# RWKV in lockstep: the results of four pairs kept in SBUF up to their group norms, and the recurrences placed later among the dense products

## The chip, the cores and the metric

The kernel runs on one core of a Trainium2 chip. Its engines work side by side, each through its own queue in order: PE (TensorE, the matmuls; its weight loads are a separate row, PEld), DVE (VectorE), ACT (ScalarE), POOL (GpSimd) and SP (SyncE, which here only issues DMA transfers). PE's clock has two levels, 1.2 and 2.4 GHz; the trace gives the granted clock as a share of the higher one. The metric is the device time of one execution in microseconds (us).

## The reference

A sequence of 512 tokens of width 1024 passes a first network of two layers and then this block: RWKV-7 and a chunked state-space mixer (SSD) side by side, gates that merge the two, and a mixture of 32 experts. The change lies in the RWKV mixer. Its core, cut:

```python
def rwkv7_mix(p, ...):                      # 16 heads of 64
    ...                                     # r, k, v, decay w, kk, a, gate g
    def step(state, inp):
        r_t, w_t, k_t, v_t, kk_t, a_t = inp
        sa = jnp.einsum('bhij,bhj->bhi', state, -kk_t)
        state = (state * w_t[:, :, None, :]
                 + sa[..., None] * (kk_t * a_t)[:, :, None, :]
                 + v_t[..., None] * k_t[:, :, None, :])
        return state, jnp.einsum('bhij,bhj->bhi', state, r_t)
    _, ys = lax.scan(step, state0, xs)
    y = jnp.moveaxis(ys, 0, 1)
    mean = jnp.mean(y, axis=-1, keepdims=True)            # group norm, per head
    var = jnp.mean(jnp.square(y - mean), axis=-1, keepdims=True)
    y = ((y - mean) * lax.rsqrt(var + RWKV_GN_EPS)).reshape(B_, S_, RWKV_WIDTH)
    y = y * ln_g + ln_b
    bonus = jnp.sum(r_h * k_h * r_k, axis=-1, keepdims=True) * v_h
    return (y + bonus.reshape(B_, S_, RWKV_WIDTH)) * g

def second_block(x, ...):
    proj = rmsnorm(x, attn_norm_g) @ w_in
    y_a, y_b = rwkv7_mix(...), ssd_mix(...)
    gates = jax.nn.sigmoid(p_gate)                        # g_a, g_b
    x = x + (g_a * (y_a @ w_up_rwkv) + g_b * (y_b @ w_up_ssd)) @ w_out
    x = x + hier_moe(rmsnorm(x, ffn_norm_g), ...)         # 32 experts, top 2
    return rmsnorm(x, final_norm_g)
```

## The kernel before

Stages of the program, by the trace's time: the first network up to about 1290 us; the two mixers (class Mix) to 2133; the merge, which multiplies their results with w_up_ssd and w_up_rwkv and then w_out, to 2330; the experts to the end.

**What a dense product is.** All activations lie transposed, 128 channels x 512 tokens. A dense product of 128 output channels is 24 matmuls of 128x512 on the rows L219 to L221 (three for each of eight slices: the operands are split into a high and a low part, on ACT, L174 and L177, and DVE, L175 and L178). Its raw weights come by a DMA of 512 KB (L193, tile wr). A gate product (G, function gate) is one such product, then DVE and ACT (L1367, L1368) and a store of gates.

**Mix.run** walks the string PLAN (L788), one step after the other: L, T set-ups; A and B, the two preparations of a pair of RWKV heads (prep1, prep2; each head pair is 128 channels, eight pairs in all); C, the recurrence of four pairs at once (chain; C0 for pairs 0 to 3, C4 for 4 to 7); P, preparation of a group of SSD heads; U, an SSD unit; V, an SSD unit with a gate product set between its parts; G, a gate product; F, fetching ahead for the merge of w_up_ssd's weights and of SSD's results (tile yr, multiplied by rs on POOL, then split as x on ACT and DVE). From this program order a scheduler makes each engine's order by dependences and free buffers, so neighbouring steps are interleaved. Inside chain, PE's own order is written by hand (manual_schedule).

**A preparation's result** is tile CH (one buffer), which prep2 stores to the DRAM scratch ch (2304 KB, L1068). GA, another tile, holds products of prep1's Gram matrices for prep2.

**chain** (L1070) runs two halves, a and b, of two pairs each, in turn through eight chunks of 64 tokens. Each half and chunk loads its slice of ch into a tile CS (576 KB, four buffers, L1095), runs groups of eight 64x64 matmuls (L1090), copies out U (L1107) and SA (L1115), and makes the next state S (L1127). The chunk's output is copied on ACT to the tile ye (L1130) and stored to DRAM as yraw (L1131).

**close** (L1133), four times behind the chain, is the group norm of one pair: y is loaded back from yraw (L1139), PE sums it over each head with the matrix bdones (L1142), DVE subtracts the mean (L1143), ACT squares into gs (L1145), PE sums again (L1147), ACT takes the root (L1149), DVE the reciprocal (L1150), two DVE steps apply ln_g, ln_b and the bonus bo (L1151, L1152; bo is loaded at L1140), then gs takes the gate g from DRAM (lora, L1154), POOL multiplies (L1155), and the result is stored as ya (L1156). The buffers of each tile are numbers in the table SB2; y and gs have one each, PSUM's cb, which both sums use, has one.

Of the kernel before, what the change touches and what calls it, by code (L numbers as in the profile page):

```python
# [8 lines left out]
F32 = mybir.dt.float32  # L9
# [681 lines left out]
AR, GK, GB, VT, BT, KT, MM = (slice(a, a + n) for a, n in ((0, 128), (128, 128), (256, 64), (320, 64), (384, 64), (448, 64), (512, 64)))  # L691
# [29 lines left out]
def pack2(x):  # L721
# [7 lines left out]
    for n in ("w_up_rwkv", "w_up_ssd", "rwkv_w_decay", "rwkv_w_a", "rwkv_w_g"):  # L729
# [5 lines left out]
    return I  # L735


SB2 = dict(k=1, r=1, v=1, L=1, E2=1, th=1, kk=1, kp=1, bo=2, y=1, gs=1, eC=3,
           CH=1, CS=4, GA=1, inv=5, N=1, M=1, Tt=1, tmp=2, U=2, SA=2, S=4, Se=2, ye=3,
           bg=5, x=2, z=1, gt=1, bt=1, xdt=1, xw=1, prev=1, G=3, e=1, ys=1, acc=1, selp=2, tp=2)  # L740
PS2 = dict(d=2, ga=2, X=1, cb=1, sb=2)

# [42 lines left out]
    return r  # L785


PLAN = "L0 L1 T A0 L2 P B0 V V A1 U B1 U P A2 V B2 V A3 U B3 V P C0 A4 V B4 U V A5 B5 U P A6 V B6 V A7 B7 U U G G C4 G G G F G F G F"  # L788


ON = dict(kk1="a", kkn="v", kp1="a", kp2="v", b="v", bK="v", inv="v", NB="a", Se="v", yg="p", cv="a", G0="v", G1="v",
# [3 lines left out]
class Mix:  # L795


    def __init__(self, K, norm, V, coef, scr, ya, yb, rs, gates):
        self.K, self.nc, self.norm, self.V = K, K.nc, norm, V
        self.ya, self.yb, self.rs, self.gates = ya, yb, rs, gates  # L800
        nc, I = K.nc, K.I
        two = (128, 2, 64)
        K.place(bg=(128, 512), bt=(128, 512), gt=(128, 512), y=(128, 512), gs=(128, 512), bo=(128, 512),
                kp=(128, 512), U=two, SA=two, S=two, Se=two, ye=two)
        K.place(CH=(128, 8, 576), CS=(128, 2, 576), GA=(128, 8, 64))
        def cst(name, shape, src=None):
            t = K.c(name, shape)
            nc.sync.dma_start(t, I["c_" + name] if src is None else src)
            return t
        self.bdones = cst("bdones", (128, 128))  # L810
        self.gmask = cst("gmask", (128, 128))
        self.lev = cst("lev", (128, 3, 64))
        self.id16 = cst("id16", (64, 256))
        self.scr = scr
        for n, t in coef.items():
            setattr(self, n, t)
        self.gps = []
        for i in range(2):
            t = K.c(f"gp{i}", (128, 514))
            nc.vector.memset(t[:, 0:1], 0.0)  # L820
            self.gps.append(t)
        self.gqs = []
        for i in range(2):
            t = K.c(f"gq{i}", (128, 515))
            nc.vector.memset(t[:, 0:3], 0.0)
            self.gqs.append(t)
        self.E1 = K.c("E1", (128, 8, 65))
        nc.vector.memset(self.E1[:, :, 0:1], 1.0)


        self.ch = [K.dr.tile([8, 2, 128, 2, 576], F32, name=f"ch{i}") for i in range(2)]
        self.eC = [[K.c(f"eC{i}{j}", (128, 2, 8)) for j in range(2)] for i in range(2)]
        self.yr = [K.dr.tile([4, 128, 512], F32, name=f"yraw{i}") for i in range(2)]
        self.bon = K.dr.tile([1024, 512], F32, name="bonus")
        self.lo = [K.dr.tile([1024, 512], F32, name=f"lora{i}") for i in range(3)]

# [93 lines left out]
    def prep1(self, p):  # L930
# [38 lines left out]
        self.proj(16 + p, ev("v", 16 + p))  # L969
        CH = P["CH"] = K.t("CH", (128, 8, 576))  # L970
        for i in range(2):
# [14 lines left out]
    def prep2(self, p, P):  # L986


        K, nc = self.K, self.nc
        CH, E2, th, kp, v = (P[n] for n in ("CH", "E2", "th", "kp", "v"))  # L990
# [17 lines left out]
                for a in range(2):  # L1008
                    self.scaled("tr", t[part(h), :, a, :], ps[part(a), :, part(h)])
        nc.vector.tensor_mul(th, th, E2)  # L1010
        GA = K.t("GA", (128, 8, 64))
        for i in range(2):
            ps, c4 = gram(th, i), slice(4 * i, 4 * i + 4)
            nc.vector.tensor_mul(GA[:, c4, :], ps[:, :, 0:64], gm[:, :, 0:64])
# [5 lines left out]
        N = K.t("N", (64, 16, 16))  # L1020
# [6 lines left out]
        M = K.t("M", (64, 16, 16))  # L1027
        nc.vector.tensor_copy(M, self.id16.rearrange("p (s t) -> p s t", s=16))
        for t in range(15, 0, -1):
            n = 16 - t  # L1030
# [4 lines left out]
        Tt = K.t("Tt", (64, 16, 16))  # L1035
# [34 lines left out]
    def chain(self, G):  # L1070


        with self.K.tc.manual_schedule(engines={mybir.EngineType.PE}):
            a, b = self.half(G, 0), self.half(G, 1)
            for c in range(8):
                for g in (a, b, a, a, b, a, b, b) if c else (a, a, a, b, a, b, b):
                    next(g)
            next(b)
        for n in range(4):
            self.close(4 * G + n)  # L1080

    def half(self, G, g):

        K, nc = self.K, self.nc
        part = lambda h: slice(h * 64, h * 64 + 64)
        def mm(o, st, mv, start=False, stop=False):
            for n in range(2):
                for h in range(2):
                    q = part(h)
                    nc.tensor.matmul(o[q, n, :], st[q, n, :], mv[q, n, :], start=start and not n, stop=stop,  # L1090
                                     skip_group_check=True)
        two = (128, 2, 64)
        for c in range(8):
            x = K.t("CS", (128, 2, 576))
            nc.sync.dma_start(x, self.ch[G][c, g])  # L1095
            at = lambda s: x[:, :, s]
            ARA, ARR, GKA, GKR = (at(slice(n, n + 64)) for n in (0, 64, 128, 192))
            eC = self.eC[G][g][:, :, c:c + 1].to_broadcast([128, 2, 64])

            X, Y = (K.p(t, (128, 2, 2, 64)) for t in (("cb", "X"), ("d", "d"))[g])  # L1100
            mm(X[:, 0], GKA, at(VT), True, not c)
            if c:
                mm(X[:, 0], ARA, S, stop=True)
            if c < 7:
                mm(X[:, 1], at(KT), at(VT))
            U = K.t("U", two)
            nc.vector.tensor_copy(U, X[:, 0])  # L1107
            yield
            mm(Y[:, 0], at(VT), GKR, True)
            if c:  # L1110
                mm(Y[:, 0], S, ARR)
            yield
            mm(Y[:, 1], at(MM), U, stop=True)
            SA = K.t("SA", two)
            nc.vector.tensor_copy(SA, Y[:, 1])  # L1115
            yield
            if c < 7:
                mm(X[:, 1], at(BT), SA, stop=True)
            mm(Y[:, 0], SA, at(GB), stop=True)
            if c < 7:  # L1120
                Sn = K.t("S", two)
                if c:
                    Se = K.t("Se", two)
                    nc.vector.tensor_add(Se, X[:, 1], S)
                    nc.vector.tensor_mul(Sn, Se, eC)
                else:
                    nc.vector.tensor_mul(Sn, X[:, 1], eC)  # L1127
                S = Sn
            y = K.t("ye", two)
            nc.scalar.copy(y, Y[:, 0])  # L1130
            nc.sync.dma_start(self.yr[G][2 * g:2 * g + 2, :, c * 64:(c + 1) * 64].rearrange("n p t -> p n t"), y)  # L1131
            yield

    def close(self, p):

        K, nc, V = self.K, self.nc, self.V
        col = lambda t: t[:, p:p + 1]
        y, bo = K.t("y"), K.t("bo")
        nc.sync.dma_start(y, self.yr[p // 4][p % 4])  # L1139
        nc.sync.dma_start(bo, self.bon[p * 128:(p + 1) * 128, :])  # L1140
        ps = K.p("cb")
        nc.tensor.matmul(ps, self.bdones, y, start=True, stop=True)  # L1142
# [10 lines left out]
        g = K.t("gs")  # L1153
# [903 lines left out]
```

## Time and profile before

| what | value |
|---|---|
| median of three runs | 2842.55 us (2842.48 to 2857.47) |
| the profiled execution, whole | 2841.89 us |
| its span in the trace | 2840.1 us |
| mean granted clock of PE | 0.978 |
| PE busy in the span | 2677.9 us (94%) |
| DVE, ACT, POOL busy | 60%, 37%, 7% |
| DMA moved | 504.44 MB, 178 GB/s on average |

A row of the timeline has the start, the duration, the engine, the line of the kernel, the operation and its tiles (out<-in), and in brackets how long the engine stood idle before it and what released it. DMA rows on SPq are the issue only, not the transfer. The windows give busy time of each engine in a stretch, the granted clock (1.00 is 2.4 GHz), the mean busy share of the 16 DMA engines, and what they moved.

### The profile page before, as it was taken

Reading aid. Unit: us, or ns where it says so; the run is one execution under the profiler, and the core shown is the slowest. Engines: PE = TensorE matmul, PEld = TensorE weight load, DVE = VectorE, ACT = ScalarE, POOL = GpSimd, SP = SyncE. Lnnn points to the kernel's source line nnn. Section 1 sums busy time; section 2 is a strip of 40 time slices with the busy share of each in tenths; the row PEclk is TensorE's granted clock in tenths of the full one; section 3 lists DMA queues with packets and bytes.
Section 4 is the critical chain, followed back from the end, with each engine's and each line's share of the span. In section 5 each row is a group of like instructions: output and inputs, shape, how many; then the busy total and the mean of one; then the engine's idle time right before and its main releaser. Section 6 shows DMA issues by size and latency. Waiting matters only on the chain. (4 is left out here: it accounts for less than half of the span.)

```text
span 2840.1 us, 40647 instructions
## 1 busy us (share of the span) xinstructions
PE 2677.9 (94%) x15658; PEld 1972.5 (69%) x15658; DVE 1702.9 (60%) x3103; ACT 1037.0 (37%) x1889; POOL 194.0 (7%) x262
## 2 busy tenths in 40 slices
PE   8989999999999999998999979999759987999997
PEld 6779888888888788885777767777637752344333
DVE  7665666645666666548787848888445442344334
ACT  4354443333344433335555526554233220110002
POOL 3100000000000000013000000000013011101000
PEclk9999999999999999999999989999979998999999
DMA  5324222223234232334434464444647839999997
GB/s 180 90 75 146 70 90 97 97 95 106 97 122 131 67 97 97 104 104 156 159 102 155 138 200 123 130 153 131 214 138 260 297 114 366 419 420 420 420 421 303
DMA packets 204692, 504.44 MB, mean 178 GB/s; under 512 B 91184, under 2 KB 92272, under 8 KB 179920
## 3 DMA queue, kind: packets, MB, share of 16 engines
q1 hardware_dynamic: 201888, 492.53, 49.1%
q0 software_dynamic: 2608, 9.28, 0.8%
q8 instruction: 124, 2.03, 0.3%
q14 instruction: 72, 0.59, 0.1%
HBM read 447.50 MB, written 54.25 MB: 177 GB/s over the span
## 5 line engine op out<-in xcount | busy, mean ns | idle before, releaser
L174 ACT CAST w<-wr 128x512 fp32r<-128x512 f32 x662 | 408.1, 620 | 727.7 <-PE ps_d L220 600.6
L219 PE MATMUL ps_d<-x,w 128*128 128x512 f32 x1624 | 651.0, 401 | 1.2 <-ACT w L174 1.1
L221 PE MATMUL ps_d<-x,w 128*128 128x512 f32 x1624 | 641.5, 395 | 2.9 <-DVE w L175 2.9
L175 DVE TENSOR_TENSOR w<-wr,w 128x512 fp32r<-128x512 f32 x662 | 470.1, 714 | 284.6 <-ACT w L174 274.2
L220 PE MATMUL ps_d<-x,w 128*128 128x512 f32 x1624 | 640.6, 394 | 0.0
L221 PEld LDWEIGHTS ps_d<-x,w 128*128 128x128 f32 x1624 | 305.7, 188 | 69.9 <-DVE w L175 4.2
L219 PEld LDWEIGHTS ps_d<-x,w 128*128 128x128 f32 x1624 | 305.9, 188 | 69.6 <-issue 7.3
L220 PEld LDWEIGHTS ps_d<-x,w 128*128 128x128 f32 x1624 | 305.8, 188 | 67.4 <-issue 6.9
L1818 PE MATMUL ps_g<-we,X 128*64 128x512 f32 x1024 | 239.9, 597 | 12.0 <-DMA we<-in_w_exp_gate 6.1
L219 PE MATMUL ps_d<-s,w 128*128 128x512 f32 x512 | 202.8, 396 | 0.0
L221 PE MATMUL ps_d<-s,w 128*128 128x512 f32 x512 | 202.6, 396 | 0.0
L220 PE MATMUL ps_d<-s,w 128*128 128x512 f32 x512 | 202.5, 396 | 0.0
L1818 PEld LDWEIGHTS ps_g<-we,X 128*64 128x64 f32 x1024 | 75.8, 137 | 160.9 <-issue 135.7
L1855 PE MATMUL ps_y<-we,hT 128*64 128x512 f32 x512 | 120.6, 600 | 0.9 <-DMA we<-in_w_exp_down 0.6
L220 PEld LDWEIGHTS ps_d<-s,w 128*128 128x128 f32 x512 | 96.1, 188 | 23.4 <-DVE s L175 0.8
L219 PEld LDWEIGHTS ps_d<-s,w 128*128 128x128 f32 x512 | 96.1, 188 | 22.7
L221 PEld LDWEIGHTS ps_d<-s,w 128*128 128x128 f32 x512 | 96.1, 188 | 22.7
L219 PE MATMUL ps_a<-x,w 128*128 128x512 f32 x232 | 91.0, 400 | 5.9 <-ACT x L1471 3.0
L220 PE MATMUL ps_a<-x,w 128*128 128x512 f32 x232 | 91.6, 396 | 0.1
L1875 DVE TENSOR_TENSOR h<-h,ps_x 128x512 f32<-128x512 f32 x128 | 81.7, 681 | 14.9 <-PE ps_x L1873 13.9
L221 PE MATMUL ps_a<-x,w 128*128 128x512 f32 x232 | 90.4, 391 | 0.0
L1855 PEld LDWEIGHTS ps_y<-we,hT 128*64 128x64 f32 x512 | 36.6, 137 | 73.8 <-issue 67.2
(557 smaller groups left out, 3939.6 us busy)
## 6 DMA issues: line engine op xcount, KB each, us to landing
we<-in_w_exp_gate SPq DMA_DIRECT2D x64, 1024.0 KB, 21.0
we<-in_w_exp_up SPq DMA_DIRECT2D x64, 1024.0 KB, 19.9
we<-in_w_exp_down SPq DMA_DIRECT2D x64, 1024.0 KB, 21.1
wr<-in_w_in SPq DMA_DIRECT2D x83, 512.0 KB, 3.7
wr<-in_ffn_w_up SPq DMA_DIRECT2D x64, 512.0 KB, 3.4
ch<-CH SPq DMA_DIRECT2D x8, 2304.0 KB, 8.2
CS<-ch SPq DMA_DIRECT2D x32, 576.0 KB, 5.1
wr<-in_ffn_w_down SPq DMA_DIRECT2D x32, 512.0 KB, 3.4
```

Source lines behind the costliest of these rows:

```text
L174: nc.scalar.copy(hi, x)
L175: nc.vector.tensor_sub(lo, x, hi.bitcast(F32))
L219: nc.tensor.matmul(ps, whi, xhi, start=start, stop=False)
L220: nc.tensor.matmul(ps, whi, xlo, start=False, stop=False)
L221: nc.tensor.matmul(ps, wlo, xhi, start=False, stop=stop)
L1818: self.nc.tensor.matmul(ps[e * 64:e * 64 + 64, :], X[:, k, e * 64:e * 64 + 64], w(e, i, k), start=(k == 0), stop=(k == 7))
L1855: nc.tensor.matmul(py[e * 64:e * 64 + 64, :], hT[:, f, e * 64:e * 64 + 64], w(e, 2, f, d), start=(f == 0), stop=(f == 3))
L1875: nc.vector.tensor_add(a, a, ps)
```

## The change

y becomes one tile of 128 x 4 x 512 that the chain's copies on ACT write and that the four closes read, so that the tile ye, the DRAM scratch yraw, its 32 stores and its 8 reloads are gone. GA is now the part MM of CH. To make room, bo has one buffer for two and S three for four. In PLAN, C0 stands one preparation and one unit with a gate product later, A7 comes ahead of V, and C4 stands behind five gate products, not two; of F, the three steps now stand last.

```diff
--- before.py
+++ after.py
@@ -735,8 +735,8 @@
     return I
 
 
-SB2 = dict(k=1, r=1, v=1, L=1, E2=1, th=1, kk=1, kp=1, bo=2, y=1, gs=1, eC=3,
-           CH=1, CS=4, GA=1, inv=5, N=1, M=1, Tt=1, tmp=2, U=2, SA=2, S=4, Se=2, ye=3,
+SB2 = dict(k=1, r=1, v=1, L=1, E2=1, th=1, kk=1, kp=1, bo=1, y=1, gs=1, eC=3,
+           CH=1, CS=4, inv=5, N=1, M=1, Tt=1, tmp=2, U=2, SA=2, S=3, Se=2,
            bg=5, x=2, z=1, gt=1, bt=1, xdt=1, xw=1, prev=1, G=3, e=1, ys=1, acc=1, selp=2, tp=2)
 PS2 = dict(d=2, ga=2, X=1, cb=1, sb=2)
 
@@ -785,7 +785,7 @@
     return r
 
 
-PLAN = "L0 L1 T A0 L2 P B0 V V A1 U B1 U P A2 V B2 V A3 U B3 V P C0 A4 V B4 U V A5 B5 U P A6 V B6 V A7 B7 U U G G C4 G G G F G F G F"
+PLAN = "L0 L1 T A0 L2 P B0 V V A1 U B1 U P A2 V B2 V A3 U B3 V P A4 V C0 B4 U V A5 B5 U P A6 V B6 A7 V B7 U U G G G G G C4 G G F F F"
 
 
 ON = dict(kk1="a", kkn="v", kp1="a", kp2="v", b="v", bK="v", inv="v", NB="a", Se="v", yg="p", cv="a", G0="v", G1="v",
@@ -800,9 +800,9 @@
         self.ya, self.yb, self.rs, self.gates = ya, yb, rs, gates
         nc, I = K.nc, K.I
         two = (128, 2, 64)
-        K.place(bg=(128, 512), bt=(128, 512), gt=(128, 512), y=(128, 512), gs=(128, 512), bo=(128, 512),
-                kp=(128, 512), U=two, SA=two, S=two, Se=two, ye=two)
-        K.place(CH=(128, 8, 576), CS=(128, 2, 576), GA=(128, 8, 64))
+        K.place(bg=(128, 512), bt=(128, 512), gt=(128, 512), y=(128, 4, 512), gs=(128, 512), bo=(128, 512),
+                kp=(128, 512), U=two, SA=two, S=two, Se=two)
+        K.place(CH=(128, 8, 576), CS=(128, 2, 576))
         def cst(name, shape, src=None):
             t = K.c(name, shape)
             nc.sync.dma_start(t, I["c_" + name] if src is None else src)
@@ -830,7 +830,6 @@
 
         self.ch = [K.dr.tile([8, 2, 128, 2, 576], F32, name=f"ch{i}") for i in range(2)]
         self.eC = [[K.c(f"eC{i}{j}", (128, 2, 8)) for j in range(2)] for i in range(2)]
-        self.yr = [K.dr.tile([4, 128, 512], F32, name=f"yraw{i}") for i in range(2)]
         self.bon = K.dr.tile([1024, 512], F32, name="bonus")
         self.lo = [K.dr.tile([1024, 512], F32, name=f"lora{i}") for i in range(3)]
 
@@ -1008,7 +1007,7 @@
                 for a in range(2):
                     self.scaled("tr", t[part(h), :, a, :], ps[part(a), :, part(h)])
         nc.vector.tensor_mul(th, th, E2)
-        GA = K.t("GA", (128, 8, 64))
+        GA = CH[:, :, MM]
         for i in range(2):
             ps, c4 = gram(th, i), slice(4 * i, 4 * i + 4)
             nc.vector.tensor_mul(GA[:, c4, :], ps[:, :, 0:64], gm[:, :, 0:64])
@@ -1071,15 +1070,16 @@
 
 
         with self.K.tc.manual_schedule(engines={mybir.EngineType.PE}):
-            a, b = self.half(G, 0), self.half(G, 1)
+            y = self.K.t("y", (128, 4, 512))
+            a, b = self.half(G, 0, y[:, 0:2]), self.half(G, 1, y[:, 2:4])
             for c in range(8):
                 for g in (a, b, a, a, b, a, b, b) if c else (a, a, a, b, a, b, b):
                     next(g)
             next(b)
         for n in range(4):
-            self.close(4 * G + n)
-
-    def half(self, G, g):
+            self.close(4 * G + n, y[:, n, :])
+
+    def half(self, G, g, y):
 
         K, nc = self.K, self.nc
         part = lambda h: slice(h * 64, h * 64 + 64)
@@ -1126,17 +1126,14 @@
                 else:
                     nc.vector.tensor_mul(Sn, X[:, 1], eC)
                 S = Sn
-            y = K.t("ye", two)
-            nc.scalar.copy(y, Y[:, 0])
-            nc.sync.dma_start(self.yr[G][2 * g:2 * g + 2, :, c * 64:(c + 1) * 64].rearrange("n p t -> p n t"), y)
+            nc.scalar.copy(y[:, :, c * 64:(c + 1) * 64], Y[:, 0])
             yield
 
-    def close(self, p):
+    def close(self, p, y):
 
         K, nc, V = self.K, self.nc, self.V
         col = lambda t: t[:, p:p + 1]
-        y, bo = K.t("y"), K.t("bo")
-        nc.sync.dma_start(y, self.yr[p // 4][p % 4])
+        bo = K.t("bo")
         nc.sync.dma_start(bo, self.bon[p * 128:(p + 1) * 128, :])
         ps = K.p("cb")
         nc.tensor.matmul(ps, self.bdones, y, start=True, stop=True)
```

The lines of the changed kernel are some lower: chain's matmuls stay at L1090, the copy to y is L1129, a close has its bo load at L1137, its first sum at L1139, then L1140 (subtract), L1142 (square), L1144 (second sum), L1146 (root), L1147 (reciprocal), L1148, L1149, L1151 (gs), L1152 (POOL), L1153 (ya); the store of ch is L1067, that of gates L1366.

What moves, at three places. First SP's queue around the start of C4; wr are weights, gates, rs and yb results that go to DRAM. Before:

```order
L1068 DMA ch_10958<-CH 128x8x576
L1369 DMA gates<-gt 128x512
L1357 DMA rs<-e 128x512
L193 DMA wr<-in_m_w_up_ssd 128x1024
L1095 DMA CS<-ch_10958 128x1152 x4
L1131 DMA yraw_10964<-ye 128x2x64
L1095 DMA CS<-ch_10958 128x1152
```

And of the changed kernel:

```order
L1067 DMA ch_10956<-CH 128x8x576
L1366 DMA gates<-gt 128x512
L1354 DMA rs<-e 128x512
L193 DMA wr<-in_m_w_up_ssd 128x1024
L1095 DMA CS<-ch_10956 128x1152
L1366 DMA gates<-gt 128x512
L1095 DMA CS<-ch_10956 128x1152 x2
L1366 DMA gates<-gt 128x512
L193 DMA wr<-in_m_w_up_ssd 128x1024 x3
L1366 DMA gates<-gt 128x512
L1095 DMA CS<-ch_10956 128x1152 x12
L1151 DMA gs<-lora_10964 128x512
```

Before, four loads of CS stand together behind the stores of ch, of one gate product and of rs, and each later one behind a store of yraw; now the first three stand among the stores of four gate products, and the last twelve in one row behind the fourth.

Second, PE's order where C0 begins; L1262 and L1268 belong to the SSD's preparation P, L1292 to L1311 to a unit, L999 to prep1. Before:

```order
L221 MATMUL ps_d<-x,w 128x512
L1090 MATMUL ps_cb<-CS 64x64 x8
L1090 MATMUL ps_X<-CS 64x64
L1262 MATMUL ps_sb<-ident,bg 128x128 x4
L1090 MATMUL ps_X<-CS 64x64 x3
L1090 MATMUL ps_X<-U,CS 64x64 x4
L1268 MATMUL ps_sb<-bg 128x128 x4
L1090 MATMUL ps_d<-CS 64x64 x8
L1090 MATMUL ps_cb<-SA,CS 64x64 x4
```

And of the changed kernel:

```order
L1292 MATMUL ps_sb<-ident,x 128x128 x4
L1090 MATMUL ps_cb<-CS 64x64 x8
L1090 MATMUL ps_X<-CS 64x64 x4
L999 MATMUL ps_ga<-CH,th 64x128 x6
L1300 MATMUL ps_sb<-xw,bg 128x128 x3
L1310 MATMUL ps_sb<-cshl,selr 128x512
L1311 LDWEIGHTS identb
L1311 MATMUL ps_sb<-capb,identb 128x512
L1090 MATMUL ps_X<-U,CS 64x64 x4
L1090 MATMUL ps_d<-CS 64x64 x8
```

Before, C0 begins inside the preparation P and waits behind its L1268; now it begins inside a unit and prep1 of pair 4, whose small matmuls stand between the chain's groups.

Third, DVE's order among the last closes before the merge; x and w are splits for the merge. Before:

```order
L178 SCALAR_TENSOR_TENSOR x<-yr,vec_66,x 128x512 x5
L1143 SCALAR_TENSOR_TENSOR y<-ps_cb,y 128x512
L1150 RECIPROCAL gs<-gs 128x512
L1151 SCALAR_TENSOR_TENSOR y<-y,vec_66,gs 128x512
L1152 SCALAR_TENSOR_TENSOR y<-y,vec_66,bo 128x512
L1143 SCALAR_TENSOR_TENSOR y<-ps_cb,y 128x512
L1150 RECIPROCAL gs<-gs 128x512
```

And of the changed kernel:

```order
L178 SCALAR_TENSOR_TENSOR x<-yr,vec_66,x 128x512 x3
L1147 RECIPROCAL gs<-gs 128x512
L1140 SCALAR_TENSOR_TENSOR y<-ps_cb,y 128x512
L1148 SCALAR_TENSOR_TENSOR y<-y,vec_66,gs 128x512
L178 SCALAR_TENSOR_TENSOR x<-yr,vec_66,x 128x512
L1149 SCALAR_TENSOR_TENSOR y<-y,vec_66,bo 128x512
L178 SCALAR_TENSOR_TENSOR x<-yr,vec_66,x 128x512
```

Before, the subtraction of a mean (L1143) stands behind the whole close ahead of it; now it (L1140) stands right behind the reciprocal of the close ahead.

On PE, 74 dense matmuls in a row stand directly ahead of C4's chain (13 before), and behind its last group 6, 10 and 32 dense ones between the first closes' sums (18, 7, 77, 11 and 7 before); the last two closes have none between them in either.

## Rows read from the trace of the kernel before

**Rows 1.** Windows: stretch, length, busy time of PE to POOL, clock, DMA share, GB/s.

```profile
1641.00:1696.00 55.00, 40.87 (x989) 37.92 (x983) 24.23 (x69) 8.53 (x22) 0.00 (x0) 0.84 0.74 238
1696.00:2006.00 310.00, 305.40 (x2154) 234.05 (x2154) 259.68 (x512) 163.48 (x318) 6.92 (x4) 1.00 0.43 131
2006.00:2058.00 52.00, 35.29 (x968) 32.08 (x966) 21.44 (x63) 7.31 (x19) 0.00 (x0) 0.90 0.79 260
2058.00:2133.00 75.00, 38.38 (x138) 25.02 (x133) 34.44 (x36) 26.87 (x37) 14.15 (x11) 0.73 0.41 131
2133.00:2330.00 197.00, 190.95 (x807) 147.04 (x806) 87.62 (x117) 60.44 (x100) 32.79 (x23) 0.99 0.66 229
2290.00:2310.00 20.00, 20.00 (x75) 12.32 (x74) 10.88 (x18) 7.06 (x12) 1.29 (x1) 1.00 0.00 1
2330.00:2840.00 510.00, 460.89 (x2289) 187.81 (x2288) 197.42 (x499) 57.25 (x99) 58.90 (x82) 0.97 0.95 390
```

**Rows 2.** Waits of PE from 1641 to 2140: line, releaser, total, times, longest.

```profile
PE ps_cb L1142 <- DMA y<-yraw: 32.3, 7, 15.8
PE ps_d L1090 <- DMA CS<-ch: 17.4, 6, 10.9
PE ps_cb L1147 <- ACT gs L1145: 6.5, 2, 5.0
PE ps_sb L1268 <- DVE bg L1245: 4.5, 1, 4.5
```

**Rows 3.** Timeline around the start of C4.

```profile
2002.81 0.63 PE L1048 MATMUL ps_ga<-inv 64*64 64x64 f32 x16
...
2005.45 0.38 SPq L1068 DMA_DIRECT2D ch<-CH  x1
...
2014.79 1.27 SPq L1095 DMA_DIRECT2D CS<-ch  x3
...
2020.27 1.12 PE L1090 MATMUL ps_d<-CS 64*64 64x64 f32 x16 [10.89 <-DMA CS<-ch]
```

**Rows 4.** Timeline of PE at the end of C4: its last group, dense matmuls.

```profile
2057.68 0.45 PE L1090 MATMUL ps_d<-CS,SA 64*64 64x64 f32 x8
...
2058.86 0.39 PE L219 MATMUL ps_d<-x,w 128*128 128x512 f32 x1
...
2060.91 0.39 PE L219 MATMUL ps_d<-x,w 128*128 128x512 f32 x1
```

**Rows 5.** Timeline of the closes of pairs 5, 6 and 7.

```profile
2086.55 0.63 ACT L1145 ACTIVATE gs<-y 128x512 f32<-128x512 f32 x1
...
2098.69 1.26 POOL L1155 TENSOR_TENSOR y<-y,gs 128x512 f32<-128x512 f32 x1 [3.06 <-DMA gs<-lora]
...
2105.75 2.05 PE L1142 MATMUL ps_cb<-y,bdones 128*128 128x512 f32 x2 [15.78 <-DMA y<-yraw]
...
2112.08 0.63 ACT L1145 ACTIVATE gs<-y 128x512 f32<-128x512 f32 x1 [1.42 <-DVE y L1143]
...
2115.59 3.35 DVE L1150 RECIPROCAL gs<-gs 128x512 f32<-128x512 f32 x1 [3.54 <-ACT gs L1149]
...
2119.76 0.32 SPq L1154 DMA_DIRECT2D gs<-lora  x1
...
2122.63 1.26 POOL L1155 TENSOR_TENSOR y<-y,gs 128x512 f32<-128x512 f32 x1 [7.05 <-issue]
...
2125.98 0.32 SPq L1139 DMA_DIRECT2D y<-yraw  x1
...
2128.69 2.04 PE L1142 MATMUL ps_cb<-y,bdones 128*128 128x512 f32 x2 [13.86 <-DMA y<-yraw]
...
2131.56 0.63 ACT L1145 ACTIVATE gs<-y 128x512 f32<-128x512 f32 x1 [16.00 <-DVE y L1143]
...
2133.33 1.42 PE L219 MATMUL ps_a<-x,w 128*128 128x512 f32 x1
```

**Rows 6.** Timeline of PE at the start of C0.

```profile
1650.64 2.08 PE L1268 MATMUL ps_sb<-bg 128*128 128x128 f32 x8 [4.54 <-DVE bg L1245]
...
1656.63 1.12 PE L1090 MATMUL ps_d<-CS 64*64 64x64 f32 x16 [3.92 <-DMA CS<-ch]
```

**Rows 7.** Tile bo: its transfers, from issue to landing.

```profile
DMA to landing us min/median/max: 2.0/3.6/7.0
```

## The prediction

> **What bounds the kernel now.** I read the windows first, by stage. From 1696 to 2006 us TensorE (PE) is busy 305.40 of 310 us: no wait of another engine counts there. On either side of that stretch it is not: in the first chain (C0, 1641 to 1696) it is idle 55 - 40.87 = 14.1 us, in the second (C4, 2006 to 2058) 16.7 us, between C4 and the merge (2058 to 2133) 36.6 us [rows 1]. In the first and the third the granted clock is 0.84 and 0.73, so a part of them ran at the lower of its two levels (1.2 of 2.4 GHz). From 2133 on PE is full again; behind it the experts read weights with the DMA engines full.
>
> Does time saved ahead of 2133 reach the end? In 2290 to 2310 DMA moves 1 GB/s while PE is busy all 20 us [rows 1]: the stream of expert weights has not begun, it stands behind PE's progress in the merge. So it begins earlier by what PE saves, and I count the savings one to one.
>
> Next, PE's waits in this stretch, by what ended them [rows 2]: the reload of y (seven times, 32.3 us, longest 15.8), the loads of CS (17.4, longest 10.9), the square in gs (6.5), the SSD's bg (4.5). The change is aimed at the first two. All sums are made against the profiled execution, 2841.89 us, which lies 0.7 us from the median of the runs (2842.55).
>
> **Storage, costed at nothing.** The 32 copies to ye become copies into y, same engine, same shape; 32 stores and 8 reloads go. GA's place in CH adds no buffer to wait for: CH is a single buffer already, written earlier in the same pair. S with 3 buffers holds the state of either half and the one being written. These edits hide behind PE in the full stretch; without that cover one more wait would cost one short step of DVE, under 1 us per chunk.
>
> A single bo: its load for the next close stands behind this close's addition. It is needed again one close later, and lands in 2.0 to 7.0 us, median 3.6 [rows 7]; a close took 22.9 us from its first matmul to the next one's [rows 5]. It stays hidden as long as a close takes more than about 7 us. The Trainium skill, "Trainium Kernel Development and Optimization", section Best Practices, says to double-buffer so that DMA overlaps compute, and so speaks against this edit. By that rule the load would be bare; that is the fourth rival.
>
> **The second chain's start.** PE waited 10.89 us for CS [rows 3]. The cause is distance: the store of CH was issued at 2005.45, the loads at 2014.79, and they landed at 2020.27, while 13 dense products only stood between the last preparation and the chain. Now 15 + 74 stand there, at 2.05/9 = 0.228 us each [rows 4] 20.3 us against 3.0. The loads landed 16.8 us after the preparation's last matmul (2002.81 + 0.63), so 20.3 covers them by 3 us. The wait goes. The clock of that stretch, 0.90 over 52 us [rows 1], means 10.4 us at the lower level; if 7 of them lie in the wait itself, the other 3 cost 1.5, which come back. What is late next: the fourth CS buffer's load stands on SP behind the store of the fifth gate product, whose matmuls end just as the chain begins. I estimate 2.5 us for that gate's steps on DVE and ACT, and 5.5 for the load (2014.79 to 2020.27); the chain takes (2058.1 - 2020.3)/8 = 4.7 us per chunk and needs this one about 6 us after its start: 2 us of new wait (bounds 0 and 5). The other 5.8 us idle in C4, each at most a short wait for a load, I leave. Saved: 10.9 + 1.5 - 2 = about **11** (8 to 13).
>
> **Between the chain and the merge.** Before: the chain's last matmul group starts at 2057.68 and ends near 2058.1, the merge's first stands at 2133.33 [rows 4, 5]: 75.2 us, of which 120 dense products are 27.3. Three gate products (72 dense, 16.4 us) are now ahead of the chain, and must be paid there. What remains after the chain's end is the time of four closes in a row with 48 dense products (10.9 us) between them, which cover nothing beyond the first close.
>
> How long is a close then? Before, the reload was part of it: multiplication on POOL, reload issued at 2125.98, landed for PE at 2128.69, first square a step later: 22.9 us from PE's 2105.75 to 2128.69 [rows 5]. After, y of all four pairs lies in SBUF, and the mean of the next pair is subtracted on DVE right behind this one's reciprocal. What still runs in series is gs, one buffer for both the square and the gate: from the square at 2112.08 through the reciprocal (3.35 us), the load of gs (issued 2119.76) to POOL's end at 2123.89 is 11.8 us; in the close before it, 2086.55 to 2099.95, 13.4 [rows 5]. So a close costs 12 to 14 us; I take 13, nearer the slower since splits of x stand between its steps on DVE and ACT. With the first square about 1.8 us behind the chain (a matmul and a subtraction), three closes of 13, and 1.8 us from the last square (2131.56) to the merge's first matmul (2133.33), the merge begins 42.6 us after the chain. Saved: 75.2 - 16.4 - 42.6 = **16.2**. With 11 us per close it is 22, with 18 it is 1.
>
> **The first chain.** Before: 14.1 us idle [rows 1], of which 4.54 for bg (SSD preparation, L1268) and 3.92 for CS [rows 6]; clock 0.84 over 55 us means 17.6 us at the lower level, 8.5 of them in those two waits, so the other 9 cost about 4.5; the reload waits of its closes are 2.7 (32.3 less 15.78 and 13.86 in the tail [rows 2, 5]). Sum 21.3. After: a dense gate product and a unit's start stand between P and C0, so bg and the first CS are ready early. But the chain now shares PE with the unit's first small products and the preparation's Gram products, which wait on DVE and ACT in their turn: bounds 0 and 8 us, I take 4, the length of one such wait for bg or CS in this stretch. CS loads during the chain: 3 (bounds 0 and 5.6, what is left of the 14.1 before). The four closes have one PSUM bank and one gs: 4.5 (bounds 2, as now, and 10, two long gs waits as in [rows 2]). Clock: 1. Sum 12.5. Saved: **9** (0 to 15).
>
> The sum: 2841.9 - 11 - 16.2 - 9 = **2806 us**.
>
> The Trainium skill, "DMA: Bandwidth & Descriptors", Specifications, has transfers under 512 B below line rate. The stores of y that go were in runs of 256 B, and the chain's window moves 260 GB/s at a DMA share of 0.79, against 390 at 0.95 in the experts [rows 1], which fits. By it the remaining loads of CS could land sooner; the sum would then be lower by up to the 5.8 us of short waits left in C4, which the third rival's price spans. No row shows CS without those stores.
>
> **The rivals.**
> 1. Slower: the closes stay long. gs's load, the yr and rs loads of the merge, and gate stores share SP in order, and POOL does the merge's products between the closes'. The tail gives nothing back at (75.2 - 16.4 - 3.6)/3 = 18.4 us per close; with the other 20 us used up too it decides at 25: then 2842, and at 30 us per close 2857. For: every step waits for a queue that is in order. Against: 11.8 and 13.4 are measured with just these neighbours in between. Chance 0.04 for 30 us and more, and 0.07 for 20 to 29 (2827 to 2854; most of it near 2830).
> 2. The waits move: C0 among the unit's and Gram products gains nothing, as each of them waits on a chain of DVE copies, and PE is in order. Then 2841.9 - 11 - 16.2 = 2815, with closes of 14 us 2818. Chance 0.15.
> 3. All waits go: C4 gives 13, a close takes 11 us (22), C0 gives 15: 2792. For: without the stores SP and the DMA engines are free in the chains. Chance 0.10.
> 4. The single bo is bare: 3.6 us in three closes, 11 us: 2817. Chance 0.04, since the row has it land long ahead.
> 5. It does not reach the end: the expert stream, full from about 2350, sets it, and PE's savings become waits there: 2842. The idle DMA engines at 2290 to 2310 speak against it. Chance 0.04.
>
> **How the numbers follow.** The forecast of 2806, itself good for 2796 to 2816, has 0.56. A measurement of this kernel tells 0.5%, 14.2 us, from no change; the border is 2828. Faster: the forecast, rivals 2, 3 and 4: 0.85. Same: the long closes and rival 5: 0.11. Slower: 0.04. The range goes from rival 3's 2792, less 3, to the border, 2789 to 2828; it leaves out 0.15 above and a little below.
>
> **What would show it.** In the changed kernel: no PE wait for y; PE's wait for CS at the second chain's start under 3 us (a wait of 5 or more refutes that step); square to square 12 to 14 us in the last three closes, and 43 us from the chain to the merge (over 55 speaks for rival 1); idle PE in the C0 stretch 8 to 13 us with a clock over 0.9 (14 or more: rival 2); POOL or DVE waiting for bo (rival 4); the expert loads beginning earlier by as much as the merge does, and the end with them (if not: rival 5). The prediction is wrong if a close is set by something that this trace shows only beside the reload.

## The result, and the profile after

| | before | after |
|---|---|---|
| median | 2844.95 us (4 runs) | 2802.24 us (2800.86 to 2802.73, 4 runs) |
| ratio to before | 1 | 0.984, 95% interval 0.981 to 0.987 |
| the profiled execution, whole | 2841.89 us | 2802.73 us |
| its span | 2840.1 us | 2800.9 us |
| last matmul of C4 to the merge's first | 75.2 us | 40.5 us |
| C4, first to last matmul | 51.5 us | 38.7 us |
| the merge begins at | 2133.33 us | 2092.88 us |

The changed kernel is 1.6% faster; the forecast was 2806 us, 1.3% faster. The two profiled executions differ by 39.2 us. By the time the merge begins 40.4 us have been gained, and 1.2 of them are lost behind it. So the effect lies in the stretch up to the merge's start.

The windows of the kernel after, cut at the same events as [rows 1] (stretch, length, busy time of PE to POOL, clock, DMA share, GB/s): first chain, the full stretch, second chain, chain to merge, merge, and 20 us inside the merge.

```profile
1682.50:1724.00 41.50, 36.20 (x1007) 33.21 (x1007) 23.38 (x74) 8.60 (x29) 0.00 (x0) 1.00 0.60 191
1724.00:2014.00 290.00, 282.21 (x2045) 217.53 (x2042) 240.49 (x470) 151.46 (x291) 7.11 (x4) 1.00 0.45 143
2014.00:2052.00 38.00, 32.27 (x953) 30.21 (x948) 17.39 (x60) 5.33 (x17) 0.00 (x0) 0.96 0.69 229
2052.00:2092.90 40.90, 20.62 (x72) 12.26 (x71) 27.38 (x27) 20.33 (x27) 12.63 (x11) 0.72 0.50 161
2092.90:2290.00 197.10, 192.32 (x795) 148.52 (x793) 87.56 (x116) 59.31 (x98) 34.29 (x24) 0.97 0.65 226
2250.00:2270.00 20.00, 20.00 (x75) 12.29 (x73) 11.16 (x18) 7.64 (x13) 1.30 (x1) 1.00 0.03 11
```

PE is idle 5.3 us in the first chain's window (14.1 before), 5.7 in the second's (16.7), 20.3 between chain and merge (36.6), and 7.8 in the stretch between the chains (4.6, there in 310 us). The clock of the first chain has gone from 0.84 to 1.00, of the second from 0.90 to 0.96. The DMA engines are nearly as idle in the merge as before (last row: 11 GB/s, 1 before).

PE's waits from 1641 to 2110, answering to [rows 2]:

```profile
PE ps_cb L1144 <- ACT gs L1142: 18.7, 5, 8.2
PE ps_cb L1139 <- ACT gs L1146: 4.8, 2, 3.1
PE ps_X L1090 <- issue: 4.8, 3, 2.1
...
PE ps_X L1090 <- DVE U L1107: 2.2, 1, 2.2
...
PE ps_cb L1090 <- DMA CS<-ch: 1.0, 2, 0.8
...
PE ps_d L1090 <- DMA CS<-ch: 0.3, 1, 0.3
```

The reload of y (32.3 us) does not exist any more, the waits for CS have gone from 17.4 us (and 3.8 more on the row ps_cb) to 1.3, bg's 4.5 us are gone. What is late now is the square in gs: 18.7 us, 6.5 before. The rows say who holds the square up. ACT's squares behind C4, with POOL's multiplication of the close ahead, answering to [rows 5]:

```profile
2052.90 0.63 ACT L1142 ACTIVATE gs<-y 128x512 f32<-128x512 f32 x1
...
2062.94 1.30 POOL L1152 TENSOR_TENSOR y<-y,gs 128x512 f32<-128x512 f32 x1 [284.86 <-DVE w L175]
...
2064.27 0.63 ACT L1142 ACTIVATE gs<-y 128x512 f32<-128x512 f32 x1 [0.48 <-POOL y L1152]
...
2075.30 1.26 POOL L1152 TENSOR_TENSOR y<-y,gs 128x512 f32<-128x512 f32 x1 [6.40 <-DVE x L178]
...
2076.59 0.63 ACT L1142 ACTIVATE gs<-y 128x512 f32<-128x512 f32 x1 [4.88 <-POOL y L1152]
...
2089.81 1.26 POOL L1152 TENSOR_TENSOR y<-y,gs 128x512 f32<-128x512 f32 x1 [4.31 <-DMA gs<-lora]
...
2091.11 0.63 ACT L1142 ACTIVATE gs<-y 128x512 f32<-128x512 f32 x1 [4.85 <-POOL y L1152]
...
2092.88 1.42 PE L219 MATMUL ps_a<-x,w 128*128 128x512 f32 x1
```

Each square starts within 0.04 us of the end of the multiplication before it. Square to square it is 11.4, 12.3 and 14.5 us, 12.7 in the mean. Before, the squares of [rows 5] lie 25.5 and 19.5 us apart, and the close that the prediction took for its measure 22.9 from first sum to first sum.

### The profile page after: what moved, and what is told of

It reads as the page before. It is cut to its first block, busy times and chain, and to the rows that moved or that the text cites. A ratio compares the mean times of both kernels' runs of the same rounds, so it can differ in the third digit from the quotient of the medians.

```text
span 2800.9 us, 40535 instructions
## 1 busy us (share of the span) xinstructions
PE 2674.5 (95%) x15658; PEld 1974.5 (70%) x15658; DVE 1707.7 (61%) x3103; ACT 1037.1 (37%) x1889; POOL 193.2 (7%) x262
```

## The experiments

The stages of every profiled execution, from the first and last matmul of each (us). The ends of matmuls are modelled by the profiler, so a length is good to 0.1 us. "C0 to merge" runs from C0's first matmul to the merge's first, so that it does not hold what lies ahead of C0; for the kernels with C0 at its old place it begins elsewhere and is left out. The merge's start itself moved by 3.6 us between two executions of the changed kernel, so only larger differences of it are used; C0 to merge differs by 0.1 to 0.3 us between two executions of one kernel. Each ratio is taken against runs of the kernel before on the same chip.

| kernel | C4 | chain to merge | merge begins | C0 to merge | merge to end | ratio to before (95%) |
|---|---|---|---|---|---|---|
| before | 51.5 | 75.2 | 2133.3 | | 706.8 | 1 |
| after | 38.7 | 40.5 | 2092.9 | 410.4 | 708.0 | 0.984 (0.981 to 0.987) |
| after, again (e11) | 37.4 | 40.6 | 2089.2 | 410.2 | 708.7 | 0.9854 (0.9837 to 0.987) |
| storage only (e1) | 54.3 | 37.8 | 2099.5 | | 720.0 | 0.9906 (0.9884 to 0.9928) |
| order only (e2) | 40.1 | 74.1 | 2136.4 | 454.1 | 706.1 | 0.999 (0.998 to 0.9999) |
| C0 back (e3) | 39.4 | 40.9 | 2107.4 | | 709.3 | 0.9894 (0.9872 to 0.9916) |
| C4 back (e4) | 47.6 | 43.6 | 2087.5 | 405.9 | 719.2 | 0.9866 (0.9841 to 0.9892) |
| four products ahead (e5) | 37.7 | 40.7 | 2087.1 | 404.1 | 709.0 | 0.9828 (0.9805 to 0.9851) |
| the same again (e12) | 37.5 | 41.2 | 2087.2 | 403.8 | 712.7 | 0.9834 (0.9818 to 0.9851) |
| gate buffer (e6) | 36.8 | 29.4 | 2087.9 | 405.9 | 718.0 | 0.9833 (0.9817 to 0.985) |
| gate buffer, C4 back (e7) | 46.7 | 33.6 | 2091.4 | 406.2 | 728.7 | 0.9882 (0.9865 to 0.9898) |
| stores kept (e8) | 40.3 | 41.8 | 2098.4 | 415.1 | 709.7 | 0.9862 (0.9845 to 0.9878) |
| gate buffer, F first (e9) | 37.7 | 32.8 | 2095.5 | 412.2 | 709.7 | 0.9855 (0.9839 to 0.9872) |
| gate buffer, six ahead (e10) | 37.2 | 30.2 | 2097.4 | 415.5 | 711.4 | 0.9875 (0.9858 to 0.9891) |

My theory at the start: the storage shortens the closes and with them the way from chain to merge, whatever stands among them; the order of steps removes the waits at the two chains' starts. The rival: the order carries the gain.

**Storage alone, and the order alone.** The edit of e1 (e2 is the reverse, the new PLAN in the kernel before):

```diff
-PLAN = "... V P A4 V C0 B4 U V A5 ... B6 A7 V B7 U U G G G G G C4 G G F F F"
+PLAN = "... V P C0 A4 V B4 U V A5 ... B6 V A7 B7 U U G G C4 G G G F G F G F"
```

> The changed storage (y in SBUF, GA in CH, bo 1, S 3) with the old order of steps. My theory: the storage alone shortens the closes to 11 to 15 us each, and the five gate products behind the chain (27.3 us) fit into the 40 us of the closes, so the stretch from the chain to the merge falls from 75.2 to about 42 us, 33 us saved; the 10.9 us wait for CS at the second chain's start and the first chain's waits stay. About 2808 us (2804 to 2812), nearly all of the change's gain. Rival A, the order carries the gain: with dense products and their gate stores between them the closes stay at 18 to 23 us each: 2825 to 2842. Rival B, the 32 stores of 256-byte runs had slowed the loads of CS: then the short waits in both chains (some 5 us each) go too and it is near 2800.

> The old storage with the new order of steps. My theory: the second chain's wait goes (12 us saved with the clock), the first chain gains 10 to 13, but the closes still take 22 to 23 us each behind their reloads, so the stretch from the chain to the merge stays near 75 us although 16.4 us of dense products have left it: net 6 to 9 us, about 2835 us (2830 to 2840). Rival A, the order carries the gain: closes shorter because fewer dense products stand among them, 60 us from chain to merge, about 2820 us.

With the storage alone, chain to merge is 37.8 us, although 120 dense matmuls stand there, and the merge begins 33.8 us earlier, as expected. The second chain's wait stays, and so does the first one's:

```profile
1657.73 1.12 PE L1090 MATMUL ps_d<-CS 64*64 64x64 f32 x16 [4.09 <-DMA CS<-ch]
...
2025.06 1.12 PE L1090 MATMUL ps_d<-CS 64*64 64x64 f32 x16 [14.02 <-DMA CS<-ch]
```

(timeline of e1, PE, the starts of C0 and C4). The theory holds to the merge's start, but the time missed its range (2821.7 us, 2808 expected): the kernel as a whole gains only 0.94%, because 13 us are lost behind the merge's start, on which more below. With the order alone, chain to merge stays at 74.1 us though three products have left it; PE's waits of e2 from C4's end to the merge:

```profile
PE ps_cb L1142 <- DMA y<-yraw: 42.1, 4, 14.7
PE ps_cb L1147 <- ACT gs L1145: 8.0, 3, 5.0
```

The wait for y behind C4 is 12 us more than before (30.1 of the 32.3 us in [rows 2] lie there), most of the 16.4 us that the three products covered. So the order alone is worth 0.1%, 3 us on this chip where 6 to 9 were expected. Part of what is lacking is that the closes of the first group wait for y too (4.2 us, 2.2 before; from the start of C0's last group to C4's first matmul it is 294.2 us, 288.3 after). The rival falls. The two parts' gains do not add: 0.94% and 0.1% apart, 1.6% together. By the merge's start the order adds 6.6 us to the storage's 33.8 with short closes, and with the old ones it takes 3.1 from the kernel before (single executions, whose merge starts scatter by 3.6). So the order pays only once the closes are short, but the percentages show it larger than it is, as e1 also loses more behind the merge's start.

**Each chain's place.** e3 and e4 are the changed kernel with one of the two steps put back. e4 puts F's three steps back among the gate products too, so it does not test C4's place quite alone:

```diff
-... V P A4 V C0 B4 ...      (e3)
+... V P C0 A4 V B4 ...
-U U G G G G G C4 G G F F F  (e4)
+U U G G C4 G G G F G F G F
```

> The changed kernel with C0 back ahead of A4 and V. My theory: place alone made the first chain's gain; the wait for bg (4.5 us), the wait for CS (3.9 us) and the lower clock behind them (4 us) come back: 10 to 14 us slower than the changed kernel, 2812 to 2816 us. Rival: the stores that are gone made it, by faster loads of CS and a free queue; then within 3 us of the changed kernel, 2802 to 2805 us.

> The changed kernel with C4 back behind two gate products, five behind it. My theory: the wait for CS (10 to 11 us, and 1.5 of clock) comes back, but 72 dense matmuls (16.4 us) move under the closes, whose length does not depend on them, so it is 2 to 5 us faster than the changed kernel: 2798 us (2795 to 2802); by this the place of C4 was worth nothing once the closes are short. Rival A, as in the prediction's sum, the place is worth 11 us by itself: 2813 us. Rival B, the closes get longer by the gate products among them, to 15 to 17 us each: 2804 to 2810 us.

C0's place is worth a little more than was expected: the merge begins 14.5 us later, and the waits for bg and for CS are back:

```profile
PE ps_sb L1265 <- DVE bg L1242: 4.5, 1, 4.5
PE ps_d L1090 <- DMA CS<-ch: 4.2, 1, 4.2
```

(waits of PE in e3, 1641 to 1700 us.) C4's place is another matter. Its wait is back:

```profile
2007.55 1.12 PE L1090 MATMUL ps_d<-CS 64*64 64x64 f32 x16 [9.72 <-DMA CS<-ch]
```

(timeline of e4, PE). But three products have gone under the closes, and C0 to merge is 4.5 us shorter than in the changed kernel: chain to merge is 3.1 us longer, C4 9 to 10, and 16.5 us less stand ahead of it. So the place of C4, to which the prediction gave 11 us, costs 4.5 us by the merge's start. The kernel's time, 2809.2 us, shows nothing of it and misses the theory's 2798: the merge takes 2.8 to 4.3 us longer (PE waits for gates there: DVE gt L1459, 5.6 us in place of 2.1) and the experts begin and end later. The time lies in rival B's range, but rival B's reason does not hold: the closes are 11.6, 12.5 and 11.9 us from square to square, not 15 to 17.

**One product moved, and the length that stays.** e5, run again as e12 beside the changed kernel (e11):

```diff
-U U G G G G G C4 G G F F F
+U U G G G G C4 G G G F F F
```

> The changed kernel with four gate products ahead of C4 and three behind it; the queues of the merge and the experts keep their order here. My theory: chain to merge stays at 40 to 42 us, set by the four closes and not by the 72 dense matmuls among them; one product (5.5 us) leaves the stretch ahead of the chain, and of its cover about 2 us come back as a wait for CS or for U: the merge begins 3 to 4 us earlier and the kernel is that much faster than the changed one (ratio to before 0.983). Rival, closes lengthen by the product among them: chain to merge 45 us or more and no gain.

> The changed kernel with four gate products ahead of C4 and three behind it, again: 3 to 6 us below the changed kernel on the same chip, as its merge began 5.8 us earlier before. Rival: within 2 us of it.

> The changed kernel, unaltered, beside the others on one chip: ratio to before 0.982 to 0.986, chain to merge 40 to 41 us.

Chain to merge is 40.7 and 41.2 us with 72 dense matmuls among the closes, as with 48; C0 to merge is 6.3 us shorter in both, a product (5.5) and a little more. PE waits 3.8 and 2.6 us for CS in C4 (0.8 and 0.2 with five products ahead), yet C4 is no longer for it, so the cover of four products is about enough. On one chip the medians are 2800.82 and 2805.48 us; the intervals of the ratios overlap, so that this version is faster than the changed kernel is likely, not shown.

**What sets a close.** e6 takes the gate out of gs:

```diff
-        g = K.t("gs")
+        g = K.t("CS", (128, 2, 576))[:, 0, 0:512]
```

> The changed kernel with the gate g of a close loaded into one of the four CS buffers, which are free behind the chain, in place of gs; nothing else is altered. My theory: gs as one buffer for square and gate sets the length of a close; without the gate in it the next square can follow the reciprocal's use, so a close falls from 12.7 to 7 to 9 us, and chain to merge from 40.5 to 27 to 31 us: the merge begins 10 to 13 us earlier. Rival, the splits of x and weights on ACT and DVE set it: then a close stays at 11 to 13 us and nothing changes. The end follows the merge's start, unless the merge's or experts' queues, whose order is made anew here, give some back, as the runs of the order of steps did by 11 to 12 us.

ACT's squares behind C4 in e6:

```profile
2058.92 0.63 ACT L1142 ACTIVATE gs<-y 128x512 f32<-128x512 f32 x1
...
2067.06 0.62 ACT L1142 ACTIVATE gs<-y 128x512 f32<-128x512 f32 x1
...
2076.33 0.63 ACT L1142 ACTIVATE gs<-y 128x512 f32<-128x512 f32 x1 [3.51 <-DVE y L1148]
...
2086.12 0.63 ACT L1142 ACTIVATE gs<-y 128x512 f32<-128x512 f32 x1 [0.89 <-DVE y L1148]
```

Square to square is 8.1, 9.3 and 9.8 us; the last two wait for DVE's use of the reciprocal, none for POOL. Chain to merge is 29.4 us, 11 less. So one buffer for square and gate was what set the length of a close, shown by its removal. The end does not follow (ratio 0.9833, 0.984 for the changed kernel, with intervals that overlap): C0 to merge is only 4.5 us shorter, because 8.4 us more pass between C0's last matmul and C4's first. The scheduler makes that stretch anew around shorter closes; from 1740 to 1790 PE is busy 40.66 us in e6 and 45.70 in the changed kernel:

```profile
1740.00:1790.00 50.00, 40.66 (x304) 29.32 (x303) 43.59 (x77) 19.45 (x35) 5.37 (x3) 0.93 0.28 89
```

(window of e6.) Its longest waits there are 3.9 us for a split of w (0.7 in the changed kernel) and 2.8 for tmp, both on DVE. And from the merge to the end e6 takes 10 us more.

> Both: the gate in a CS buffer, and C4 behind two gate products with five behind it (F last). My theory: the wait for CS of 9.7 us is back, 16.4 us of dense products have gone under the closes, which now need 28 us against 27.3 us of dense products: chain to merge 29 to 33 us, the merge begins 9 to 13 us earlier than in the run with C4 back alone (2087.5) and near 2076 us. Rival, PE is now the bound there and closes and dense products add up: 36 us and more from chain to merge.

> The changed kernel with the gate in a CS buffer, and one fetch (F) placed directly behind C4, ahead of the last gate products; the queues behind the merge's start are nearer to those of the changed kernel than in the first run with a gate buffer. My theory, that the run with a gate buffer gained 11 us from chain to merge and lost 10 behind it by its queues' new order: chain to merge 28 to 31 us, and less than 4 us lost behind the merge's start: 2793 to 2799 us, ratio to before 0.980 to 0.982. Rival, what comes after the merge's start takes back whatever the closes give, in any order: 2800 to 2806 us.

> The same gate buffer, with six gate products ahead of C4 and one behind it. My theory: the closes alone set chain to merge, so it stays 27 to 30 us with 24 dense matmuls less among them, and the sixth product (5.5 us) is now paid ahead of the chain: the merge begins about 5 us later than in the run with F first; 2797 to 2804 us. Rival, the dense products share the length of a close by their steps on DVE and ACT: chain to merge falls to 24 us or less and nothing is lost.

Three more orders on top of e6's edit:

```diff
-U U G G G G G C4 G G F F F
+U U G G C4 G G G G G F F F   (e7)
+U U G G G G G C4 F G G F F   (e9)
+U U G G G G G G C4 G F F F   (e10)
```

Chain to merge is 33.6 us in e7 with 27.3 us of dense products in it, a little over what was expected, and the merge begins 15 us later than expected. In e9 and e10 it is 32.8 and 30.2 us, in e10 with one product only: the closes set it, as the theory has it. But 298 and 302 us pass between the chains (288.3 after; in e10 5.5 of it are the sixth product), and neither is faster than the changed kernel: both times, 2807.8 and 2811.3 us, missed their ranges. The rival of e9 as it was put, that what follows the merge takes the gain back, fails too: merge to end is 709.7 us there. The gain was spent ahead of C4.

**The stores.** e8 adds the stores back, from y, read by nobody.

```diff
             nc.scalar.copy(y[:, :, c * 64:(c + 1) * 64], Y[:, 0])
+            nc.sync.dma_start(self.yr[G][...][:, :, c * 64:(c + 1) * 64]..., y[:, :, c * 64:(c + 1) * 64])
```

> The changed kernel with the 32 stores of each chunk's result to DRAM added back (64 KB each in runs of 256 bytes), read by nobody. My theory: the stores were next to harmless in the chains; the second chain keeps its length of 38.7 us within 1.5 us; the first close's subtraction now waits for the last stores to land, 3 to 5 us more from chain to merge. About 2806 us in all (ratio to before 0.986). Rival, stores in short runs slow the loads of CS: each chain grows by 4 us or more.

C0 to merge is 4.8 us longer. C0 takes 46.2 us (42.9 and 43.8 in the two executions without, to the start of the last group), C4 40.3 (38.7, 37.4), chain to merge 41.8 (40.5). So the stores cost 1.6 to 3.3 us in each chain, less than the rival says and more than I gave them there, and about 1 behind, where I gave them 3 to 5. Most of it is waits for CS. PE's waits of e8 from 1641 to 2110:

```profile
PE ps_cb L1091 <- DMA CS<-ch: 2.3, 3, 1.0
...
PE ps_d L1091 <- DMA CS<-ch: 1.7, 5, 0.6
```

These 4.0 us were 1.3 and 0.2 in the two executions without stores. The loads themselves are little slower. For only two of the 32 loads does e8's profile tell the landing, but the DMA packets of the trace give all of them (128 of 4608 bytes each): the median from issue to the last packet is 4.6 us with the stores, and 4.2 and 4.4 without (4.4 and 4.5 in e5 and e12). Whether the rest is a later issue, behind the store in SP's queue, no run here separates.

**What is lost behind the merge.** e1, e4, e6 and e7 take 718 to 729 us from the merge to the end, 10 and more above the changed kernel. A part of it needs no change of the kernel: e5 and e12 are one kernel, with 709.0 and 712.7. Their windows for the 10 us ahead of the router's sum and the 20 behind it, e5 and then e12:

```profile
2279.70:2289.70 10.00, 8.47 (x51) 7.09 (x50) 6.07 (x34) 5.12 (x10) 0.00 (x0) 0.83 0.60 246
2289.70:2309.70 20.00, 5.64 (x48) 5.03 (x48) 9.15 (x55) 2.05 (x4) 6.36 (x9) 0.60 0.92 358
```

```profile
2278.80:2288.80 10.00, 7.05 (x51) 5.53 (x49) 6.00 (x34) 5.17 (x10) 0.00 (x0) 0.96 0.74 299
2288.80:2308.80 20.00, 6.46 (x40) 5.91 (x40) 8.72 (x55) 2.05 (x4) 6.37 (x9) 0.50 0.78 303
```

In e12 the clock stays low through the 20 us (0.50, all at 1.2 GHz), the stores of h take 9.20 us on SP's queue (6.38 in e5), and the first expert's matmul comes 23.1 us behind the router, 20.2 in e5. Of these 2.9 us 2.4 lie at the beginning, from the router's sum (L1678) to POOL's first step behind it (L1766), e5 and then e12:

```profile
2289.69:2292.90 3.21, 2.80 (x24) 2.68 (x24) 2.65 (x19) 1.52 (x4) 0.00 (x1) 1.00 0.47 174
2288.87:2294.50 5.63, 5.22 (x24) 5.08 (x24) 2.65 (x19) 2.05 (x4) 0.00 (x0) 0.50 0.22 81
```

PE does the same 24 matmuls in 2.80 us at the higher level and 5.22 at the lower one. All fourteen profiles fall in line: this stretch takes 3.21 us at a clock of 1.00 in nine of them, 5.6 us at 0.50 in e1, e4, e6 and e12, and 4.83 us at 0.59 in e7. What brings the clock down just there is open. So is the rest of the loss of e1, e4, e6 and e7, of which the merge itself, up to the router's sum, has 2 to 14 us against the changed kernel and the experts about 5; two executions of the changed kernel differ by 1.5 and 2 us there.

## Why the prediction was right

The time, 2802 us against 2806, and its parts: C4 with what follows from its start 12.8 us (11 forecast), chain to merge 18.3 us when the 16.4 us of moved products are taken off (16.2), the rest, which is C0 and the stretch behind it, 9.3 us (9). The expert weights are loaded earlier as the merge begins earlier (the first load is issued at 2130.98 us, 2169.92 before), and the end comes earlier with it, so the fifth rival fell. The reading behind it was not right, though: in 2290 to 2310 the DMA engines were idle not because the stream had yet to begin, but after its first 13 loads, issued from 2169.92 to 2246.48; the next is issued at 2313.31. Point by point:

**The closes.** 12 to 14 us were forecast from gs's chain in [rows 5], 13 taken; 12.7 measured, and 40.5 us from chain to merge against 42.6. The mechanism, one buffer for square and gate, is shown by e6. The single closes, 11.4, 12.3 and 14.5 us, spread wider than 12 to 14. The last close is the longest (14.5 us), since its root waits on ACT behind a split of x that waits for POOL, which is the reason why 13 was taken and not 12. Rival 1 (long closes) is excluded by these numbers, in e1 too, where five products stand among them.

**The second chain.** The wait for CS went, as forecast, and 2 us of new wait came, as forecast, but not where it was put. The fourth load of CS was in time, though the fifth gate's steps took 3.6 us from its last matmul to its store's issue and not the 2.5 of the sum; PE waits 2.16 us for U, which stands on DVE behind the fifth gate product's step, and that waits until the store of gates has freed its tile:

```profile
2015.81 0.69 DVE L1364 TENSOR_TENSOR gt<-ps_d,rstd 128x512 f32<-128x512 f32 x1 [3.55 <-DMA gates<-gt]
2016.42 0.28 DVE L1107 COPY U<-ps_cb 128x128 f32<-128x128 f32 x1
2016.59 0.72 ACT L1365 ACTIVATE gt<-gt,hbg 128x512 f32<-128x512 f32 x1 [5.05 <-DVE gt L1364]
2016.76 0.45 PE L1090 MATMUL ps_X<-U,CS 64*64 64x64 f32 x8 [2.16 <-DVE U L1107]
```

(timeline of the kernel after, the start of C4.) The sum entered 11 us here and charged 16.4 us to the tail for the products that moved. Together they are right. Read singly, as I read them, they are not: e4 and e5 show that those products would have stood under the closes for little or nothing, so by the merge's start the place of C4 costs 4.5 us and does not earn 11. What was wrong is the attribution of the 11 us to C4's place, which left out that short closes still have room for the products.

**The first chain.** 12.5 us were forecast to remain of 21.3; 5.3 remain in the window and 3.2 at the four closes, and the clock is 1.00 and not a little under it. So more was saved there than forecast, 12 us or more, and about 2 us were given back elsewhere between the chains; that 9 came out is chance in part. Of the 5.3 us, 4.8 are gaps in the middle of the chain's matmuls that the profile puts down to "issue"; the last section says what stands behind them. No term of the prediction names them. Rival 2 (the waits move to the unit's and Gram products) fell: e3 shows the place to be worth 14.5 us.

**The single bo.** Nobody waits for bo in the changed kernel; its loads land in 2.0 to 3.4 us. The rule of the Trainium skill ("Trainium Kernel Development and Optimization", Best Practices: double-buffer) did not bear on bo, which is needed a close later, and does bear on gs, where a second place for the gate took 11 us off the tail (e6), though not off the whole time.

**The stores of 256 bytes.** By the Trainium skill ("DMA: Bandwidth & Descriptors", Specifications), transfers under 512 B run below line rate. The prediction took from it that its sum could be up to 5.8 us too high, by CS landing sooner. e8 gives the stores 4.8 us in all, and 2.7 to 3.8 of them are longer waits of PE for CS; but the loads themselves land only 0.1 to 0.4 us later in the median, so the rate of the short stores is not shown to be the reason.

## What to carry to other kernels

When a step that repeats is short of buffers, follow its one-buffer tile from its first writer to its last reader: that length, not the sum of its waits, was the step's period here once the longest wait was gone. A wait that is covered by moving work ahead of it is only a gain if the work had no cover where it stood; count both ends, and measure them by putting each move back alone. And an order made by a scheduler moves elsewhere when one buffer changes, so a gain is read at the next common event of the program and then at the end, and the difference of the two is looked for by stages.

## What was not expected of the hardware

One and the same kernel (e5 and e12) needed 20.2 us in one execution and 23.1 in another from the router to the first expert, and most of the difference is one short run of 24 matmuls that met the higher level of the clock in one and the lower in the other.

The gaps with "issue" as their releaser (4.8 us in the first chain of the changed kernel, 2.3 in the second) go with PE's instructions arriving late. One of them, on PE:

```profile
1706.28 0.40 PE L1090 MATMUL ps_X<-CS 64*64 64x64 f32 x8
1706.52 0.39 PE L1090 MATMUL ps_X<-CS,S 64*64 64x64 f32 x6
1709.00 0.21 PE L1090 MATMUL ps_X<-CS,S 64*64 64x64 f32 x1 [2.09 <-issue]
1709.01 0.27 PE L1090 MATMUL ps_X<-U,CS 64*64 64x64 f32 x1
1709.06 0.22 PE L1090 MATMUL ps_X<-CS,S 64*64 64x64 f32 x1
```

The group is cut after six of its eight matmuls. No records are missing: the trace has 1920 of the chains' matmuls in every run, 960 for each chain. Inside a chain the gaps stand 127, 254 or 381 matmuls apart, multiples of 127. The DMA table has a queue of its own for instructions, which moves blocks of 16384 bytes:

```profile
q8 instruction: 124, 2.03, 0.3%
```

In all fourteen profiles there are 95 such gaps of more than 0.3 us in the chains, and every one ends 1.20 to 1.62 us (1.39 in the median) after such a block has landed; here the block landed at 1707.76. So PE stands still there for want of instructions, as far as timing can show it; no run alters the loading of instructions. In rows of short 64x64 matmuls this is now the largest loss in the changed kernel's chains: 7.1 of the 11 us that PE is idle in them.
